# Modulation vectors as dot products on VectorE instead of fp32 matmuls

## The chip, the core and the metric

The kernel runs on one core of a Trainium2 chip. A core has a matrix engine (TensorE, PE in the profile, with PEld for its weight loads), three elementwise engines (VectorE or DVE, ScalarE or ACT, GpSimd or POOL) and a queue engine (SyncE or SP) that issues the DMAs here. PE reads on-chip memory (SBUF) and writes to the accumulation banks (PSUM). The metric is the device time of one execution in microseconds, lower is better.

## What is computed

Two transformer-like blocks, two layers each, over 256 tokens of 1024 features, all in fp32. The change lies in the first block, where each layer begins with six modulation vectors of 1024 per stream, of a stream `x` and a stream `ctx`:

```python
for l in range(DEPTH):                       # DEPTH = 2
    with_ctx = l < DEPTH - 1
    mod_x = (silu(c) @ w_ada[l] + b_ada[l])         # w_ada[l]: [1024, 6144]
    mod_c = (silu(c_ctx) @ w_ada[l] + b_ada[l])
    sh1, sc1, gt1, sh2, sc2, gt2 = split(mod, 6)    # of each stream
    hx = rms_norm(x, g_norm1[l]) * (1 + sc1_x) + sh1_x        # hc alike
    # q, k, v of three mixers = hx @ w_in[l], hc @ w_in[l]; attention over both streams' keys
    x = x + gt1_x * (concat(mixers a, b, c) @ w_out[l])
    hx2 = rms_norm(x, g_norm2[l]) * (1 + sc2_x) + sh2_x
    x = x + gt2_x * conv_ffn(hx2, ...)
    # and ctx likewise, if with_ctx
```

`c` and `c_ctx` are single vectors, so each modulation row is a matrix-vector product with 25 MB of weights per layer.

## The kernel before

A large product is made exact in three passes: `K.weights` (line 153) loads weight tiles of 128 x 1024 (`wraw`, five slots, one 512 KB DMA each on SP's queue, line 144) and `K.split` (255) makes a high part `wh` on ACT (line 259) and a low part `wl` on DVE (line 260); PE then runs high x high, high x low and low x high (lines 178 to 180).

The modulation rows of a layer come from `Block1.ada` (line 305). It is a generator of 24 steps: three banks of 2048 columns (`[sh1|sc1]`, `[gt1|sh2]`, `[sc2|gt2]`), eight 128-row blocks each. A step loads two `wraw` tiles and runs four fp32 matmuls of 32 columns x 512, side by side on the array (line 318; the trace shows each as two records). The stationary operand holds 16 copies of each stream's silu(c). After eight steps DVE adds the bias to the row (323), four transposes turn it into columns (343), DVE copies or scales the columns (353, 355), and gate rows are written to DRAM (326), from where `gate_rows` (360) loads them onto all partitions.

`layer` (line 753) chains the generators of both layers as `self.side`. Eight steps run at the very start, ahead of everything that needs sh1 and sc1; the others run one at a time at each `tick()`: after a 256-column chunk of the input projection (`qb kb vb`, mixer b, `qa0 qa1 kava`, mixer a, `qc kc vc`, mixer c, in the order of `STEPS`), and after each pair of heads in a mixer. All 48 steps of both layers are over before layer 0's FFN.

The program is written in this order, but a scheduler issues it: of the instructions ready on an engine it takes the one written first, by its own estimate of the times, and fixes the order of every engine at compile time. On the chip each engine works strictly in that order. Attention of a head is: scores on PE (533), row maximum on DVE (542), exp on ACT (546), reciprocal and scaling on DVE (594, 553), transposes on PE (558), copy on ACT (560), product with v on PE (574). The second norm (`norm_to`, 219) feeds the FFN through DVE and ACT (265, 268, 269).

Of the kernel before, what the change touches and what calls it, by code (L numbers as in the profile page):

```python
# [50 lines left out]
class Core:  # L51
    def __init__(self, ctx, tc):
# [100 lines left out]
    def weights(self, flat, key, layer, k0, nk, starts, width, piece=1024):  # L153
        """columns (start, k, col) of a weight block as exact (high, low) float32r parts"""
# [27 lines left out]
    def rsqrt(self, parts, n, inv_n):  # L182
        """(sum(parts) * inv_n + EPS) ** -0.5, n columns"""
# [12 lines left out]
        # a cubic step and Newton's, each short of a factor: s goes from -1 to -8/3 to 1024/27, which cancels big ** -0.5  # L196
# [58 lines left out]
    def split(self, src, h, l, gain=None, shift=None):  # L255
        """src (PSUM or SBUF, fp32) * gain + shift -> h + l."""
# [15 lines left out]
    def transpose_split(self, blocks, dsts):  # L272
        """blocks: SBUF [P, P] pieces -> dsts (h, l) [P, P * len(blocks)]"""
# [8 lines left out]
class Block1:  # L282
# [21 lines left out]

    def ada(self, l):
# [3 lines left out]
        m = self.mod[l] = {}  # L309
        gn = self.gn[:, l]  # L310
        for b in range(3):
            bias = K.tile([P, 512], F32, "bada")
            nc.sync.dma_start(bias, self.ap["bada"][l, b])
            ps = K.bank("ada")
            for k in range(KD):
                raw = K.raw(f"w1_{l}", "w_ada", l, k, 1, [b * 2048 + g * 512 for g in range(4)], 512)
                for g in range(4):
                    nc.tensor.matmul(ps[32 * g : 32 * g + 32, :], self.cT[:, k].rearrange("p s r -> p (s r)"), raw[g // 2][0][:, g % 2 * 512 : g % 2 * 512 + 512],  # L318
                                     start=(k == 0), stop=(k == KD - 1), tile_position=(0, 32 * g))
                if k < KD - 1:  # L320
                    yield
            row = K.tile([P, 512], F32, "junk")
            nc.vector.tensor_tensor(row, ps, bias, op=ALU.add)
            if b:
                self.rows[l, b] = K.dram.tile([8, 512], F32, name=f"row_{l}_{b}")
                nc.sync.dma_start(self.rows[l, b], row[0 : P : 16, :])
# [428 lines left out]
    def layer(self, l):  # L755
# [788 lines left out]
```

## Time and profile before

| what | value |
|---|---|
| device time, median of 3 runs | 2211.74 us (2209.02 to 2217.74) |
| span of the profiled execution (first to last instruction) | 2206.8 us |
| what lies around the span: median less span | 4.9 us |
| PE busy | 2121.0 us (96%) |
| DVE busy | 1491.9 us (68%) |
| ACT busy | 1073.9 us (49%) |
| DMA | 331.63 MB, mean 150 GB/s |

Busy time of an engine is the union of its instructions; matmuls are pipelined, so PE at 100% says that something was always in flight. Layer 0 of the first block takes 0 to about 760 us of the span: the first modulation rows to 31, projections and mixers to 354, the output projection to 402, the second norm to 420, the FFN to 760. Everything after that contains no modulation work.

### The profile page before, as it was taken

Reading aid. Unit: us, or ns where it says so; the run is one execution under the profiler, and the core shown is the slowest. Engines: PE = TensorE matmul, PEld = TensorE weight load, DVE = VectorE, ACT = ScalarE, POOL = GpSimd, SP = SyncE. Lnnn points to the kernel's source line nnn. Section 1 sums busy time; section 2 is a strip of 40 time slices with the busy share of each in tenths; the row PEclk is TensorE's granted clock in tenths of the full one; section 3 lists DMA queues with packets and bytes.
Section 4 is the critical chain, followed back from the end, with each engine's and each line's share of the span. In section 5 each row is a group of like instructions: output and inputs, shape, how many; then the busy total and the mean of one; then the engine's idle time right before and its main releaser. Section 6 shows DMA issues by size and latency. Waiting matters only on the chain.

```text
span 2206.8 us, 35818 instructions
## 1 busy us (share of the span) xinstructions
PE 2121.0 (96%) x14204; PEld 1859.2 (84%) x14204; DVE 1491.9 (68%) x3008; ACT 1073.9 (49%) x1841; POOL 0.8 (0%) x7
## 2 busy tenths in 40 slices
PE   6999999899999999998999999998998999998998
PEld 3785667788888898788998899998997999997997
DVE  5663556855556686678777889866555879976454
ACT  4443453532333364566556644455444654454443
POOL 0000000000000000000000000000000000000000
PEclk9998999899999998999999999999999999999999
DMA  9344555322323331034554445554553545554662
GB/s 342 110 163 138 187 189 177 136 76 97 108 77 124 104 99 53 25 123 164 176 200 160 153 163 192 191 182 145 190 184 127 172 153 163 184 190 145 189 183 76
DMA packets 94839, 331.63 MB, mean 150 GB/s; under 512 B 10928, under 2 KB 11312, under 8 KB 94544
## 3 DMA queue, kind: packets, MB, share of 16 engines
q1 hardware_dynamic: 94672, 329.35, 45.5%
q8 instruction: 111, 1.82, 0.3%
q14 instruction: 56, 0.46, 0.1%
HBM read 328.20 MB, written 1.11 MB: 149 GB/s over the span
## 4 chain that ended last, share of the span: by engine, by line
PE 91%; DVE 6%; ACT 2%; DMA 1%; issue 1%; DVEq 0%; ACTq 0%
PE ps L178 17%; PE ps L179 17%; PE ps L180 16%; PE acc L178 6%; PE acc L179 6%; PE acc L180 6%; PE ps L533 4%; PE ada L318 3%; PE o L574 2%; PE ps L558 2%; PE ada L179 1%; PE ada L178 1%; PE ada L180 1%; PE o L179 1%; PE o L178 1%; PE o L180 1%
## 5 line engine op out<-in xcount | busy, mean ns | idle before, releaser
L178 PE MATMUL ps<-T,wh 128*128 128x256 f32 (+1 forms) x2640 | 787.4, 299 | 1.1 <-ACT T L262 1.1
L179 PE MATMUL ps<-T,wh 128*128 128x256 f32 (+1 forms) x2640 | 785.8, 298 | 0.4 <-DVE T L263 0.4
L180 PE MATMUL ps<-T,wl 128*128 128x256 f32 (+1 forms) x2640 | 784.5, 298 | 0.0
L260 DVE TENSOR_TENSOR wl<-wraw,wh 128x1024 fp32r<-128x1024 f32 (+1 forms) x514 | 608.8, 1201 | 157.6 <-ACT wh L259 90.8
L259 ACT CAST wh<-wraw 128x1024 fp32r<-128x1024 f32 (+1 forms) x514 | 515.8, 1031 | 234.6 <-PE ps L179 77.4
L178 PEld LDWEIGHTS ps<-T,wh 128*128 128x128 f32 x2640 | 506.1, 192 | 18.5 <-ACT T L262 2.1
L179 PEld LDWEIGHTS ps<-T,wh 128*128 128x128 f32 x2640 | 506.4, 192 | 17.3 <-DVE T L263 1.3
L180 PEld LDWEIGHTS ps<-T,wl 128*128 128x128 f32 x2640 | 506.2, 192 | 13.8
L178 PE MATMUL acc<-wh,T 128*128 128x256 f32 (+1 forms) x988 | 314.2, 319 | 3.5 <-ACT T L265 3.1
L179 PE MATMUL acc<-wl,T 128*128 128x256 f32 (+1 forms) x988 | 313.1, 318 | 2.3 <-DVE wl L260 2.3
L180 PE MATMUL acc<-wh,T 128*128 128x256 f32 (+1 forms) x988 | 311.5, 316 | 0.3 <-DVE T L269 0.3
L178 PEld LDWEIGHTS acc<-wh,T 128*128 128x128 f32 x988 | 190.3, 193 | 19.4 <-ACT T L265 3.5
L180 PEld LDWEIGHTS acc<-wh,T 128*128 128x128 f32 x988 | 189.9, 192 | 14.7 <-DVE arena L189 1.3
L179 PEld LDWEIGHTS acc<-wl,T 128*128 128x128 f32 x988 | 190.6, 193 | 13.9 <-DVE wl L260 3.0
L542 DVE TENSOR_REDUCE arena<-ps 128x1 f32<-128x512 f32 (+1 forms) x100 | 67.5, 686 | 78.9 <-PE ps L533 78.5
L1141 DVE SCALAR_TENSOR_TENSOR arena<-arena 128x241 f32<-128x241 f32 (+14 forms) x240 | 113.2, 474 | 3.7
L259 ACT CAST T<-arena 128x256 fp32r<-128x256 f32 (+2 forms) x128 | 58.8, 468 | 96.3 <-PE ps L179 26.7
L533 PEld LDWEIGHTS ps<-T,T 128*128 128x128 f32 (+2 forms) x320 | 59.3, 200 | 54.1 <-issue 29.2
L533 PE MATMUL ps<-T,T 128*128 128x256 f32 (+2 forms) x320 | 100.9, 386 | 2.1 <-ACT T L517 2.1
L318 PE MATMUL ada<-wraw,arena 128*32 128x512 f32 x384 | 86.9, 636 | 11.6 <-DVE arena L293 8.3
L546 ACT ACTIVATE arena<-ps,arena 128x512 f32<-128x512 f32 (+1 forms) x120 | 73.6, 620 | 48.1 <-DVE arena L542 37.5
L260 DVE TENSOR_TENSOR T<-arena,T 128x256 fp32r<-128x256 f32 (+2 forms) x128 | 63.2, 501 | 48.8 <-ACT T L259 48.4
(226 smaller groups left out, 2219.1 us busy)
## 6 DMA issues: line engine op xcount, KB each, us to landing
wraw<-w SPq DMA_DIRECT2D x586, 512.0 KB, 4.0
wraw<-w SPq DMA_DIRECT2D x22, 256.0 KB, 2.9
xo<-row SPq DMA_DIRECT2D x12, 256.0 KB, 6.2
v<-xin SPq DMA_DIRECT2D x4, 512.0 KB, 8.5
arena<-rpb SPq DMA_DIRECT2D x8, 256.0 KB, 2.7
v<-post SPq DMA_DIRECT2D x4, 512.0 KB, 4.4
arena<-bada SPq DMA_DIRECT2D x6, 256.0 KB, 5.4
arena<-bc SPq DMA_DIRECT2D x2, 768.0 KB, 4.0
```

Source lines behind the costliest of these rows:

```text
L178: mm(out, ah, bh, start=start, stop=False)
L179: mm(out, ah, bl, start=False, stop=False)
L180: mm(out, al, bh, start=False, stop=stop)
L259: a = nc.scalar.copy(h, src)
L260: b = nc.vector.tensor_tensor(l, src, h.bitcast(F32), op=ALU.subtract)
L318: nc.tensor.matmul(ps[32 * g : 32 * g + 32, :], self.cT[:, k].rearrange("p s r -> p (s r)"), raw[g // 2][0][:, g % 2 * 512 : g % 2 * 512 + ...
L533: self.nc.tensor.matmul(ps[:, col : col + 256], a[:, c], b, start=(n == 0), stop=(n == len(q[s]) - 1))
L542: nc.vector.tensor_reduce(m, ps.rearrange("p (t k) -> p t k", t=nt), axis=AX, op=ALU.max, negate=True)
L546: nc.scalar.activation(p[:, c], ps[:, c], AF.Exp, bias=m[:, i : i + 1], accum_out=tot[:, i : i + 1])
L558: nc.tensor.transpose(ps[:, b * P : b * P + P], p[:, b * P : b * P + P], K.ident)
L574: self.nc.tensor.matmul(out[64 * i : 64 * i + 64, t * P : t * P + P], v[:, k, cols[i] : cols[i] + 64], pts[i][:, b * P : b * P + P], start ...
L1141: yield v.scalar_tensor_tensor(y[:, lo:hi], zs[j][:, lo + t - 15 : hi + t - 15], self.cfw[:, j, t : t + 1], y[:, lo:hi], op0=ALU.mult, op1 ...
```

## The change

The first shift and scale of layer 0 stay fp32 matmuls (`ada_first`, eight steps). All other modulation values are dot products on DVE: the weights are laid out so that 128 outputs lie on the partitions and the 1024 inputs along the row, silu(c) and silu(c_ctx) are broadcast to all partitions once (`crow`), and one `scalar_tensor_tensor` (line 351 of the changed file) multiplies a 128 x 1024 weight tile with a row and writes the 128 sums as a column (`accum_out`). Its product goes to a scratch tile that nobody reads.

```diff
+    def crows(self):
+        self.crow = K.tile([P, 2, D], F32, "crow")
+        nc.sync.dma_start(self.crow, self.ap["crow"].partition_broadcast(P))
+        nc.scalar.activation(self.crow, self.crow, AF.Silu)
...
+    PARTS = dict(sh1=0, sc1=8, gt1=16, sh2=24, sc2=32, gt2=40)
     def ada(self, l):
-        for b in range(3):
-            ps = K.bank("ada")
-            for k in range(KD):
-                raw = K.raw(f"w1_{l}", "w_ada", l, k, 1, [b * 2048 + g * 512 for g in range(4)], 512)
-                for g in range(4):
-                    nc.tensor.matmul(ps[32 * g : 32 * g + 32, :], self.cT[:, k]..., raw[g // 2][0][...], ...)
-                yield
...
+        for name, b0 in self.PARTS.items():
+            if name in m or (name == "sc1" and "a1" in m):
+                continue
+            streams = (0, 1) if l == 0 or name in ("sh1", "sc1") else (0,)
+            for b in range(b0, b0 + 8):
+                ((w, _),) = K.raw(f"w1_{l}", "w_ada_t", l, b, 1, [0], D)
+                for s in streams:
+                    nc.vector.scalar_tensor_tensor(K.tile([P, D], F32, "unread"), w, 1.0, self.crow[:, s],
+                                                   op0=ALU.mult, op1=ALU.mult, accum_out=vals[s][:, b : b + 1])
+                if b == b0 + 7:
+                    for s in streams:
+                        self.part(l, name, s, vals[s][:, b0 : b0 + 8], gn)
+                yield
+    def part(self, l, name, s, v, gn):
+        b0 = self.PARTS[name]
+        nc.vector.tensor_tensor(v, v, self.badac[l][:, b0 : b0 + 8], op=ALU.add)
+        if name[:2] == "gt":
+            row = self.rows[l, int(name[2]), s] = K.dram.tile([1, D], F32, ...)
+            nc.sync.dma_start(row.rearrange("o (b p) -> p (o b)", p=P), v)
+            return
...
@@ layer
-            self.side = chain(*(self.ada(i) for i in range(self.depth)))
-            front = [K.normed(self.x[0]), None]
-            for _ in range(KD):
-                self.tick()
+            front = [K.normed(self.x[0]), None]
+            self.ada_first()
+            self.crows()
+            self.side = chain(*(self.ada(i) for i in range(self.depth)))
@@ layer, FFN of layer 0
                 for j in part:
                     F[j] = self.ffn_up(l, j, XT, n)
+                    self.tick()
+                    self.tick()
```

`part` adds the bias (`badac`, laid as columns); a gate's column goes to DRAM as a row of 1024 (line 366 of the changed file), from where `gate_rows` loads it onto all partitions as before.

A step is now one tile of 128 outputs: 32 steps for layer 0 (two dot products each) and 48 for layer 1 (16 with two, 32 with one), 128 dot products in all. The 38 ticks of the mixers of layer 0 take the first 38 steps, 76 dot products; the ticks in the FFN take the others. Weight bytes are the same as before.

The instructions move as follows. DVE, ahead of the first row maximum of mixer a: `L465`, `L466` and the `L453` to `L462` group are the norm and rope of q and k, `L209` to `L211` the steps of a reciprocal square root. Before, these rows follow each other up to there:

```order
L466 TENSOR_TENSOR xo_1498<-arena,xo_1498 128x8x64
L211 SCALAR_TENSOR_TENSOR arena<-arena 128x8
L465 TENSOR_TENSOR arena<-arena 128x512
L466 TENSOR_TENSOR xo_1517<-arena,xo_1517 128x8x64
L459 TENSOR_TENSOR arena<-arena 128x4x32
L460 TENSOR_TENSOR arena<-arena 128x4x32
L453 TENSOR_REDUCE arena<-arena 128x4
L461 TENSOR_TENSOR arena<-arena 128x256
```

In the changed kernel the last rows ahead of that maximum (`L576`) are (`L351` are dot products, the `L499` and `L500` rows the old `L465` and `L466`):

```order
L1013 TENSOR_SCALAR arena<-arena 128x124
L210 SCALAR_TENSOR_TENSOR arena<-arena 128x4
L351 SCALAR_TENSOR_TENSOR arena<-wraw_2065,arena 128x1024
L211 SCALAR_TENSOR_TENSOR arena<-arena 128x4
L1015 TENSOR_SCALAR arena<-arena 128x32
L351 SCALAR_TENSOR_TENSOR arena<-wraw_2065,arena 128x1024
L499 TENSOR_TENSOR arena<-arena 128x256
L351 SCALAR_TENSOR_TENSOR arena<-wraw_2109,arena 128x1024
L500 TENSOR_TENSOR xo_1657<-arena,xo_1656 128x256
L351 SCALAR_TENSOR_TENSOR arena<-wraw_2109,arena 128x1024
L351 SCALAR_TENSOR_TENSOR arena<-wraw_2149,arena 128x1024
L576 TENSOR_REDUCE arena<-ps_1686 128x1
```

Dot products have come in between. Counted over the whole order, 19 of them stand ahead of the first maximum of mixer b, 24 more ahead of that of mixer a (one of them among mixer b's own rows), 28 more ahead of that of mixer c (7 among mixer a's rows) and 5 more ahead of the first weight split of the output projection. The other DVE rows between these marks are nearly those of before.

DVE in the second norm of layer 0 (`L232` scales x, `L189` to `L202` the reciprocal square root, `L268` and `L269` the modulated splits that the FFN waits for). Before:

```order
L232 TENSOR_SCALAR xo_3904<-arena 128x512
L200 SCALAR_TENSOR_TENSOR arena<-arena 128x1
L201 SCALAR_TENSOR_TENSOR arena<-arena 128x1
L202 SCALAR_TENSOR_TENSOR arena<-arena 128x1
L232 TENSOR_SCALAR xo_3973<-v_307_2887,arena 128x512
L191 SCALAR_TENSOR_TENSOR arena<-arena 128x1
L323 TENSOR_TENSOR arena<-ada_3131,arena 128x512
L268 TENSOR_SCALAR arena<-ps_3905,arena 128x256
```

and after the change:

```order
L197 TENSOR_SCALAR arena<-arena 128x1
L362 TENSOR_TENSOR arena<-arena 128x8
L202 SCALAR_TENSOR_TENSOR arena<-arena 128x1
L198 SCALAR_TENSOR_TENSOR arena<-arena 128x1
L232 TENSOR_SCALAR xo_3791<-v_274_2759,arena 128x512
L199 SCALAR_TENSOR_TENSOR arena<-arena 128x1
L362 TENSOR_TENSOR arena<-arena 128x8
L351 SCALAR_TENSOR_TENSOR arena<-wraw_4017,arena 128x1024
L268 TENSOR_SCALAR arena<-ps_3723,arena 128x256
```

Of the row add of the third bank (`L323`) nothing is left, and six dot products stand between the first reciprocal square root and the last split.

SP's queue between the weight tiles of `vb` and those of `qa0`. Before, `wraw_711` and `wraw_713` are one modulation step, 721 and 723 `vb`, 912 to 961 two modulation steps:

```order
L144 DMA wraw_711<-w_0 128x1024
L144 DMA wraw_713<-w_0 128x1024
L144 DMA wraw_721<-w_0 128x1024
L144 DMA wraw_723<-w_0 128x1024
L144 DMA wraw_912<-w_0 128x1024
L144 DMA wraw_914<-w_0 128x1024
L144 DMA wraw_959<-w_0 128x1024
L144 DMA wraw_961<-w_0 128x1024
L588 DMA arena<-rpb 128x512
```

After the change 715 and 717 are `vb`, 906 to 1140 seven tiles for dot products, 1146 and 1148 `qa0`:

```order
L144 DMA wraw_715<-w_0 128x1024
L144 DMA wraw_717<-w_0 128x1024
L144 DMA wraw_906<-w_0 128x1024
L144 DMA wraw_949<-w_0 128x1024
L144 DMA wraw_993<-w_0 128x1024
L144 DMA wraw_1040<-w_0 128x1024
L144 DMA wraw_1083<-w_0 128x1024
L144 DMA wraw_1127<-w_0 128x1024
L144 DMA wraw_1140<-w_0 128x1024
L144 DMA wraw_1146<-w_0 128x1024
L144 DMA wraw_1148<-w_0 128x1024
```

A tile's slot comes free when DVE has used it, so the loads of `qa0` stand behind the dot products.

## Rows read from the trace of the kernel before

**Rows 1.** The profile page, span, busy times, the chain that ended last

```profile
span 2206.8 us, 35818 instructions
...
PE 2121.0 (96%) x14204; PEld 1859.2 (84%) x14204; DVE 1491.9 (68%) x3008; ACT 1073.9 (49%) x1841; POOL 0.8 (0%) x7
...
PE 91%; DVE 6%; ACT 2%; DMA 1%; issue 1%; DVEq 0%; ACTq 0%
PE ps L178 17%; PE ps L179 17%; PE ps L180 16%; PE acc L178 6%; PE acc L179 6%; PE acc L180 6%; PE ps L533 4%; PE ada L318 3%; PE o L574 2%; PE ps L558 2%; PE ada L179 1%; PE ada L178 1%; PE ada L180 1%; PE o L179 1%; PE o L178 1%; PE o L180 1%
```

**Rows 2.** Windows of all engines, busy us by stretch, clock, DMA

```profile
core 0: us, PE busy (x) PEld busy (x) DVE busy (x) ACT busy (x) POOL busy (x), PEclk, DMA share, GB/s
0.00:31.00 31.00, 17.90 (x91) 5.43 (x92) 9.90 (x74) 9.92 (x19) 0.84 (x7) 1.00 0.94 359
31.00:84.00 53.00, 49.25 (x368) 43.37 (x366) 38.59 (x120) 31.56 (x58) 0.00 (x0) 0.94 0.45 166
84.00:122.00 38.00, 37.73 (x250) 20.94 (x249) 21.60 (x55) 19.92 (x49) 0.00 (x0) 1.00 0.59 204
122.00:168.00 46.00, 43.61 (x354) 40.38 (x351) 31.01 (x104) 19.61 (x37) 0.00 (x0) 1.00 0.40 137
168.00:256.00 88.00, 87.93 (x495) 46.85 (x495) 35.35 (x92) 38.14 (x95) 0.00 (x0) 0.90 0.44 145
256.00:299.00 43.00, 42.65 (x375) 40.53 (x370) 25.82 (x77) 21.54 (x44) 0.00 (x0) 1.00 0.60 205
299.00:354.00 55.00, 52.89 (x300) 27.13 (x298) 34.29 (x115) 30.13 (x85) 0.00 (x0) 1.00 0.66 214
354.00:402.00 48.00, 47.13 (x392) 46.50 (x396) 35.19 (x90) 10.86 (x18) 0.00 (x0) 1.00 0.35 114
402.00:420.00 18.00, 8.61 (x53) 6.26 (x45) 16.12 (x63) 12.96 (x30) 0.00 (x0) 0.66 0.70 235
420.00:760.00 340.00, 340.00 (x1497) 281.15 (x1497) 202.71 (x276) 131.06 (x166) 0.00 (x0) 1.00 0.31 99
```

**Rows 3.** Windows of line 318 alone, the fp32 modulation products

```profile
31.00:84.00 53.00, 4.69 (x16) 0.62 (x16) 0.94 0.45 166
84.00:122.00 38.00, 9.25 (x56) 1.36 (x56) 1.00 0.59 204
122.00:168.00 46.00, 3.46 (x21) 0.45 (x18) 1.00 0.40 137
168.00:256.00 88.00, 24.55 (x102) 3.29 (x102) 0.90 0.44 145
256.00:299.00 43.00, 2.13 (x16) 0.31 (x16) 1.00 0.60 205
299.00:354.00 55.00, 26.28 (x96) 3.58 (x96) 1.00 0.66 214
```

**Rows 4.** Groups by form, count, busy us, mean ns, idle before

```profile
L260 DVE TENSOR_TENSOR wl<-wraw,wh 128x1024 fp32r<-128x1024 f32 x494 | 595.6, 1222 | 154.0 <-ACT wh L259 90.8 <-PE ps L180 27.6 <-issue 12.5
...
L546 ACT ACTIVATION_READ_ACCUMULATOR arena<-ps,arena 128x1 f32 x120 | 24.4, 203 | 0.0
...
L260 DVE TENSOR_TENSOR wl<-wraw,wh 128x512 fp32r<-128x512 f32 x20 | 13.5, 687 | 3.6 <-PE ps L180 2.8 <-PE acc L179 0.7
...
L641 DVE SCALAR_TENSOR_TENSOR arena<-arena 128x512 f32<-128x512 f32 x16 | 11.9, 744 | 0.1
```

**Rows 5.** Timeline of DVE, start us, us, instruction [idle before <-releaser]

```profile
29.96 0.69 DVE L323 TENSOR_TENSOR arena<-ada,arena 128x512 f32<-128x512 f32 x1 [1.62 <-PE ada L318]
...
426.01 3.49 DVE L260 TENSOR_TENSOR wl<-wraw,wh 128x1024 fp32r<-128x1024 f32 x3
```

**Rows 6.** Timeline of PE, first projection and first scores of mixer a

```profile
34.43 0.58 PE L178 MATMUL acc<-wh,T 128*128 128x256 f32 x1 [3.07 <-ACT T L265]
...
167.12 0.89 PE L512 MATMUL ps<-ident_r,xo 128*128 128x128 f32 x6 [1.65 <-ACT xo L486]
```

**Rows 7.** Windows after that 1.65 us gap

```profile
170.00:185.00 15.00, 15.00 (x37) 6.07 (x37) 5.73 (x14) 3.12 (x8) 0.00 (x0) 0.50 0.43 141
```

More of the change, by code (lines that the diff above doesn't have):

```diff
@@ L303, in load_small, with ada_first @@
         self.sm = {k: sm[:, a:b] for k, (a, b) in SM1.items()}
+    def ada_first(self):
+        K, nc = self.K, self.nc
+        gn = self.gn[:, 0]
+        bias = K.tile([P, 512], F32, "bada")
+        nc.sync.dma_start(bias, self.ap["bada"])
+        ps = K.bank("ada")
+        for k in range(KD):
+            raw = K.raw("w1_0", "w_ada", 0, k, 1, [g * 512 for g in range(4)], 512)
+            for g in range(4):
+                nc.tensor.matmul(ps[32 * g : 32 * g + 32, :], self.cT[:, k].rearrange("p s r -> p (s r)"), raw[g // 2][0][:, g % 2 * 512 : g % 2 * 512 + 512],
+                                 start=(k == 0), stop=(k == KD - 1), tile_position=(0, 32 * g))
+        row = K.tile([P, 512], F32, "junk")
+        nc.vector.tensor_tensor(row, ps, bias, op=ALU.add)
+        v = self.ada_cols(row)
+        self.mod[0] = dict(sh1=self.mod_col(v[:, 0:2]), a1=self.mod_col(v[:, 2:4], gn[:, 0:8]))
@@ new lines, in crows @@
+    def crows(self):
+        K, nc = self.K, self.nc
+        self.crow = K.tile([P, 2, D], F32, "crow")
+        nc.sync.dma_start(self.crow, self.ap["crow"].partition_broadcast(P))
+        nc.scalar.activation(self.crow, self.crow, AF.Silu)
+        self.badac = []
+        for l in range(self.depth):
+            self.badac.append(K.tile([P, 48], F32, "badac"))
+            nc.sync.dma_start(self.badac[l], self.ap["badac"][l])
+    PARTS = dict(sh1=0, sc1=8, gt1=16, sh2=24, sc2=32, gt2=40)
@@ L305, in ada @@
     def ada(self, l):
         K, nc = self.K, self.nc
[L309 removed]
+        m = self.mod.setdefault(l, {})
         gn = self.gn[:, l]
[L311 to L334 removed]
@@ new lines, in ada @@
+        vals = [K.tile([P, 48], F32, "adav") for _ in range(2)]
+        for name, b0 in self.PARTS.items():
[5 more added lines that the diff above has]
+                for s in streams:
+                    nc.vector.scalar_tensor_tensor(K.tile([P, D], F32, "unread"), w, 1.0, self.crow[:, s], op0=ALU.mult, op1=ALU.mult,
+                                                   accum_out=vals[s][:, b : b + 1])
+                if b == b0 + 7:
+                    for s in streams:
+                        self.part(l, name, s, vals[s][:, b0 : b0 + 8], gn)
+                yield
@@ new lines, in part @@
+    def part(self, l, name, s, v, gn):
+        K, nc = self.K, self.nc
+        b0 = self.PARTS[name]
+        nc.vector.tensor_tensor(v, v, self.badac[l][:, b0 : b0 + 8], op=ALU.add)
+        if name[:2] == "gt":
+            row = self.rows[l, int(name[2]), s] = K.dram.tile([1, D], F32, name=f"row_{l}_{name}_{s}")
+            with nc.allow_non_contiguous_dma(reason="a column to a row"):
+                nc.sync.dma_start(row.rearrange("o (b p) -> p (o b)", p=P), v)
+            return
+        if name[:2] == "sc":
+            nc.vector.scalar_tensor_tensor(v, v, 1.0, gn[:, 0:8] if name == "sc1" else gn[:, 8:16], op0=ALU.add, op1=ALU.mult)
+        self.mod[l].setdefault("a" + name[2] if name[:2] == "sc" else name, []).append(v)
@@ L362, in gate_rows @@
         out = K.xo()
-        for j in range(2):
-            a = 2 * (2 * (n - 1) + j) + s
-            self.nc.sync.dma_start(out[:, j * 512 : j * 512 + 512], self.rows[l, n][a : a + 1, :].to_broadcast([P, 512]))
+        self.nc.sync.dma_start(out, self.rows[l, n, s].to_broadcast([P, D]))
         return out
@@ L852, in layer @@
             K.norm_to(self.x[s], XT, s * 256, mod["a2"][s], mod["sh2"][s], site=f"n2{l}")
-        for _ in self.side:
-            pass
-        gates = {s: self.gate_rows(l, 2, s) for s in streams}
+        gates = {}
         if full:
@@ L873, in layer @@
                         self.add_gated(self.x[t // 2][t % 2][:, cc * 512 : cc * 512 + 512], ps[t], gates[t // 2][:, cc * 512 : cc * 512 + 512])
+            for _ in self.side:
+                pass
         else:
+            gates = {0: self.gate_rows(l, 2, 0)}
             ps = dict(zip([(t, cc) for t in tts for cc in range(2)], K.acc4()))
@@ L1479, in _pack @@
         if (key, layer) not in done:
-            w = inputs["w_in_2" if key == "w_kr_2" else key][layer]
+            w = inputs[{"w_kr_2": "w_in_2", "w_ada_t": "w_ada"}.get(key, key)][layer]
+            if key == "w_ada_t":
+                w = w.T
             done[key, layer] = w[:, perms[key]] if key in perms else w
@@ L1512 @@
     arrays["gn"] = np.stack([np.concatenate([_cols(i["g_norm1"][l], KD), _cols(i["g_norm2"][l], KD)], axis=1) for l in range(2)], axis=1)
-    arrays["bada"] = np.stack([np.repeat(i["b_ada"][l].reshape(3, 4, 1, 512), 32, axis=2).reshape(3, P, 512) for l in range(2)])
+    arrays["bada"] = np.repeat(i["b_ada"][0, :2048].reshape(4, 1, 512), 32, axis=1).reshape(P, 512)
+    arrays["badac"] = np.stack([_cols(i["b_ada"][l], 48) for l in range(2)])
+    arrays["crow"] = np.concatenate([i["c"][0], i["c_ctx"]])
     arrays["rpb"] = np.stack([_rpb_tiles(i["rpb_b"][l]) for l in range(2)])
```

12 lines of the change are left out of this document (3 added, 9 removed).

## The prediction

> **What bounds the kernel now.** I read the page first. PE is busy for 2121.0 of 2206.8 us, and the chain that ended last is 91% PE, 6% DVE [rows 1]; the reader is to see that `ada L318`, the work removed, is 3% of that chain, some 66 us. Next the windows by stage, since 96% is an average: from 31 us to the output projection at 354 PE is busy for 313.2 of 323 us (49.25 + 37.73 + 43.61 + 87.93 + 42.65 + 52.89), DVE for 186.7 (38.59 + 21.60 + 31.01 + 35.35 + 25.82 + 34.29), and in the FFN PE is busy for all of 340.00 us and DVE for 202.71 [rows 2]. Line 318 by itself has 70.4 us there, 4.69 + 9.25 + 3.46 + 24.55 + 2.13 + 26.28 [rows 3]. Last the forms and timelines, for prices. The profiled execution lasted 2206.8 us between first and last instruction; the measured median is 4.9 us more, and I add these 4.9 to a span. The PE order behind layer 0's FFN is the same in both kernels, so all that changes lies before 760 us.
>
> **What goes.** PE loses 70.4 us between 31 and 354 us, which leaves 313.2 − 70.4 = 242.8, and about 2 us more in the output projection and the second norm, where PE waits for DVE and ACT anyway (8.61 busy of 18.00 us [rows 2]).
>
> **The price of a dot product.** The trace shows no DVE instruction that accumulates. The nearest row is a product of two fp32 tiles by the same instruction at half the length, 744 ns for 128x512; a DVE pass of the other kind costs 687 at 512 columns and 1222 at 1024, so 512 columns more are 535, and 744 + 535 = 1279 ns [rows 4]. Packed densely, three such passes take 3.49 us, 1.163 each [rows 5] instead of 1.222, so 1279 − 59 = 1220 is the lower end. If the sum is written by a second instruction, the nearest row is the readout of ACT's accumulator, 203 ns [rows 4]: 1279 + 203 = 1482 is the upper end. I take 1.35 us, in the middle, since rows on DVE and on ACT are about equally far from it.
>
> One rule speaks against this price. The Trainium skill, "Vector Engine (DVE) Microarchitecture Reference", section "Points that are easy to get wrong", says that this instruction with two SBUF sources that aren't bf16 runs at half throughput, as no read port is left for the accumulator. The row of 744 ns has two fp32 SBUF sources and is 57 ns over the 687 of a plain pass, so no halving shows where nothing is accumulated; with accumulation no run here shows it. It is a rival below.
>
> **What it adds, stage by stage.** 76 dot products fall in 31 to 354 us: 76 × 1.35 = 102.6 on DVE, 289 with the 186.7, against 243 of PE. By sums alone DVE would still fit into 323 us. But DVE works in order, and the dot products stand ahead of the row maxima that PE's scores, exp and transposes hang on. So the bound moves to DVE in the stretches ahead of a mixer, and to PE inside one. The stages (ends of before: 31, 84, 122, 168, 256, 299, 354):
>
> - Front. `crow` (128 × 2048 × 4 bytes, 1 MB) and another 0.5 MB tile now go to the queue ahead of the last projection tile, and the layer's small table of 0.35 MB (688 columns) goes behind it: 1.05 + 0.52 − 0.35 = 1.22 MB at the 359 GB/s that the front shows [rows 2] is 3.4 us. PE's first projection product, at 34.43 [rows 6], comes some 3 us later; I start DVE at 34.
> - To the first maximum of mixer b (19 dot products): DVE 38.6 + 19 × 1.35 = 64.3, and 3 us of waits for PE and ACT, to 101 (84 before).
> - Mixer b: PE 37.7 − 9.25 = 28.5. Before mixer a the granted clock stands at 0.50, the lower of its levels (1.2 GHz), for 15 us [rows 7] after a stretch of thin PE work that ends with a wait of only 1.65 us [rows 6]. Longer waits ahead of mixers b and a make such a fall likely in each; I add 7 us, half of that stretch being lost. Against it DVE runs free while PE works off mixer b and does some 8 us of the next stage's rows. 27.5, to 128.5.
> - To the maximum of mixer a (1 + 23 dot products): DVE 31.0 + 23 × 1.35 = 62.1, to 190.5 (168 before).
> - Mixer a: PE 87.93 − 24.55 = 63.4, 8 of DVE's run-ahead off as above, 55.4, to 246. The 7 dot products in its rows are covered, DVE being busy for 35.35 of 88.
> - To the maximum of mixer c (21): DVE 25.8 + 28.4 = 54.2, to 300 (299 before).
> - Mixer c and projection chunk tail: DVE 34.3 + 5 × 1.35 = 41, with 3 us of waits, 44; PE has 52.9 − 26.3 = 26.6 and is covered. To 344 (354 before): 10 us won.
> - Output projection: 3 dot products beside 47 us of PE, covered. DVE has 35.19 there [rows 2]; with 4 more it still fits.
> - Second norm: six dot products in the chain, 6 × 1.35 = 8.1, less the row add of 0.69 [rows 5] and 1.9 of idle that they fill: 5.5 lost. This one stands in the open, PE having nothing else.
> - FFN: 43 × 1.35 = 58 on DVE, 261 of 340 us, where PE is busy for all 340 [rows 2]. Splits of weights come a little late at times; 2 us, from 0 to 8 (8 is six dot products met by PE without cover).
>
> Sum: −10 + 5.5 + 2 = −2.5 against 2206.8, a span of 2204.3, and with 4.9 about 2209 us. Beside these, ACT's pass over `crow` lies in the front, where ACT has 9.92 of 31 us [rows 2], and the bias adds take 8 columns where the old row add had 512 (0.69 us [rows 5]): I take 0 for both, and at most that 0.69 for each of the four adds ahead of the maxima if they find no gap. The gate's row, written from a column in 1024 pieces of 4 bytes, is no row of this trace. Its readers come after mixer c, a stage of 55 us [rows 2] that hides it; I take 0, and 7 if the weights queued behind it on SP are held up.
>
> The sum says: PE gives up 72 us, DVE's queue takes 70 of them back. What is least sure is the overlap, so both sides stay open.
>
> **The rivals.**
> 1. Faster. The dot product costs the lower end, 1.22, and fills the gaps between the short norm and rope instructions, where DVE is idle for 136 us (323 − 186.7). Then the three stretches ahead of the maxima shrink by 63 × 0.13 = 8 us, the two clock losses or waits (7 and 3) vanish, and the second norm loses 4.5 instead of 5.5; with another 7 us of run-ahead, 2209 − 8 − 10 − 1 − 7 = 2183. For it: that idle time is 42% of the mixers. Against it: idle time between dependent short instructions is only filled by what stands there in the order.
> 2. PE stays the bound everywhere, all of the 70.4 are won and the second norm costs nothing: 2140. Against it: DVE's own sum ahead of each maximum is longer than PE's.
> 3. Slower, by one mechanism: DVE as an in-order queue, with no run-ahead during mixers b and a, since the next chunk's tiles wait for `wraw` slots that dot products hold on SP. The two overlaps of 8 us are lost: 2209 + 16 = 2225, past the half per cent by themselves. With 1.48 a dot product ahead of the maxima (63 × 0.13 = 8) and 8 instead of 2 us in the FFN it is 2239, and with the 1.3 of the second norm about 2240. It decides if the first maximum of mixer a comes later than 195 us. For it: before, a split of `qa0` never stood behind a dot product. Against it: five slots, and loads at 45% of the DMA [rows 2].
> 4. A dot product runs at half speed, its accumulation taking turns with its reads: of the 1279 ns, 2 × 535 grow with the columns, and twice that gives 1279 + 1070 = 2349 ns. 73 of the dot products stand where DVE sets the end (63 + 5 + 5 and over), 73 × 1.0 = 73 more: about 2282. For it: no row accumulates on DVE, so none excludes it. Against it: 744 beside 687 [rows 4], two such sources at nearly the speed of a plain pass. (This is what the rule cited from the Trainium skill, "Vector Engine (DVE) Microarchitecture Reference", section "Points that are easy to get wrong", would do here.)
>
> **How the numbers follow.** A measurement of this kernel tells about 0.5%, 11 us, from no change. The forecast has 0.38 (own range 2190 to 2225), rival 1 0.27, rival 2 0.06, rival 3 0.23, rival 4 0.06. The range leaves out rivals 2 and 4 and the outer edges of 1 and 3: 2168 to 2250. Faster than 2201: rivals 1 and 2 and a little of the forecast's lower side, 0.36. Slower than 2223: rivals 3 and 4 with a bit of the forecast, 0.30. Between: 0.34.
>
> **What the profile after would show.** Right: a mean of line 351 between 1.22 and 1.48 us; PE waits that end with DVE ahead of the first maxima, these at about 101 and 190 us, the output projection from about 344; a granted clock under 1 in mixers b and a; a longer PE gap at the second norm; PE still full in the FFN. Wrong: a mean under 1.2 or over 1.5; the first maximum of mixer b before 90 us (rival 1 or 2); PE waits that end with DMA, which the working above has only at the front; or an FFN longer than 348 us, where the dot products there would not be covered.

## The result

The changed kernel takes 2227.5 us (median, 2222.07 to 2230.27); the kernel before took 2210.47 beside it (2208.9 to 2217.74). The ratio is 1.0067, 95% interval 1.0046 to 1.0088: slower, by 17 us. The forecast was 2209. What has to be found is where the 72 us of PE work went that the change takes away.

The page of the changed kernel answers to [rows 1]:

```profile
span 2220.3 us, 35410 instructions
...
PE 2087.5 (94%) x13864; PEld 1879.1 (85%) x13864; DVE 1615.8 (73%) x3268; ACT 1071.0 (48%) x1842; POOL 0.8 (0%) x7
...
PE 83%; DVE 11%; ACT 2%; DMA 2%; issue 2%; SPq 0%; DVEq 0%; ACTq 0%
```

PE has lost 33.5 us of busy time (2121.0 − 2087.5), not 72, and DVE has 11% of the chain instead of 6%. The same stretches as in [rows 2], now of the changed kernel (columns as there):

```profile
31.00:84.00 53.00, 41.53 (x289) 37.08 (x286) 47.38 (x153) 27.01 (x50) 0.00 (x0) 0.81 0.60 211
84.00:122.00 38.00, 34.22 (x213) 28.80 (x211) 29.25 (x67) 20.20 (x42) 0.00 (x0) 0.87 0.47 125
168.00:256.00 88.00, 74.92 (x446) 53.60 (x445) 62.43 (x166) 44.45 (x110) 0.00 (x0) 0.83 0.25 74
299.00:354.00 55.00, 39.25 (x162) 33.92 (x162) 34.49 (x106) 26.15 (x73) 0.00 (x0) 0.50 0.24 60
402.00:420.00 18.00, 12.21 (x94) 12.01 (x94) 17.86 (x68) 7.12 (x18) 0.00 (x0) 0.85 0.20 55
420.00:760.00 340.00, 331.87 (x1454) 273.80 (x1453) 251.74 (x371) 129.75 (x169) 0.00 (x0) 0.98 0.52 161
```

The reader is to look at the third column from the end, the granted clock of TensorE (1.00 is 2.4 GHz, 0.50 is 1.2 GHz). In 299 to 354 us, where it was 1.00 before, it is 0.50, and PE is busy for 39.25 us with 162 instructions, where it did 300 in 52.89. Over the whole program the mean clock fell. Of the changed kernel:

```profile
core 0: 2220.3 us, clock 0.950
```

and of the kernel before:

```profile
core 0: 2206.8 us, clock 0.976
```

(1 − 0.976) × 2206.8 = 53 us of full-speed time were withheld before, (1 − 0.950) × 2220.3 = 111 us now, 58 us more. The loss lies ahead of 760 us, where the mean fell from 0.98 to 0.90; behind that it is 0.98 in both. Of the 72 us that PE gave up, the clock took back up to 58: an upper bound, since a part of the withheld time falls into PE's waits.

The stages are read from the first row maximum of each mixer (DVE) and from PE: the first product of the projections, the first high x low product behind mixer c's last product with v (column "out. proj."; single products of the output projection can stand earlier, between the heads of mixer c), and the first product of the FFN. One profile each, in us:

| kernel | first product | max b | max a | max c | out. proj. | FFN | span |
|---|---|---|---|---|---|---|---|
| before | 34.4 | 85.9 | 169.7 | 300.0 | 354.8 | 419.9 | 2206.8 |
| forecast | 37.9 | 101 | 190.5 | 300 | 344 | 414.5 | 2204.3 |
| after | 42.5 | 102.8 | 188.7 | 302.2 | 364.7 | 432.6 | 2220.3 |
| e1_row | 43.5 | 102.6 | 189.4 | 303.4 | 359.8 | 427.8 | 2215.4 |
| e2_warm | 45.5 | 106.2 | 190.3 | 303.5 | 367.6 | 436.7 | 2225.9 |
| e3_both | 45.5 | 104.4 | 188.4 | 301.9 | 358.3 | 427.4 | 2216.7 |
| e4_short | 42.2 | 104.6 | 196.6 | 303.7 | 349.6 | 393.6 | 2185.8 |
| e5_short_row | 41.7 | 95.7 | 179.7 | 287.7 | 333.6 | 381.6 | 2172.3 |
| e6_late | 42.7 | 93.7 | 188.3 | 330.4 | 401.2 | 465.4 | 2258.7 |
| e7_late_crow | 34.3 | 85.1 | 175.5 | 315.2 | 386.0 | 450.2 | 2243.4 |
| e8_warm_pt | 43.9 | 102.7 | 189.5 | 309.5 | 363.5 | 424.9 | 2212.0 |
| e9_split | 35.8 | 86.7 | 170.9 | 282.2 | 328.8 | 395.3 | 2184.0 |
| e10_early | 36.0 | 87.4 | 171.2 | 296.9 | 340.0 | 393.2 | 2181.0 |
| e11_row_crow | 35.8 | 95.1 | 181.5 | 297.6 | 355.2 | 420.3 | 2208.2 |
| e12_row_crow_warm | 34.1 | 92.3 | 184.3 | 300.4 | 359.3 | 416.8 | 2204.4 |
| e13_cap26 | 34.1 | 93.0 | 180.1 | 290.8 | 332.3 | 387.1 | 2180.2 |

(The forecast's FFN is 344 plus the 65.0 us from output projection to FFN of before plus 5.5.) Up to mixer c the forecast holds within 2.2 us at each maximum. From there to the output projection it had 44 us, and 62.5 passed. What PE waits for (timeline of the changed kernel's PE, [rows 6] before):

```profile
42.46 0.58 PE L178 MATMUL acc<-wh,T 128*128 128x256 f32 x1 [5.06 <-ACT wh L259]
...
314.05 0.80 PE L178 MATMUL acc<-wh,T 128*128 128x256 f32 x2 [8.18 <-ACT wh L259]
...
316.39 1.97 PE L686 MATMUL o<-v,arena 128*128 128x64 f32 x8 [0.69 <-ACT arena L594]
```

Two waits stand out: 5.06 us ahead of the first projection, and 8.18 us in mixer c, both for ACT. The product that waits in mixer c is one of the output projection; it stands between the heads in PE's fixed order, so the heads behind it wait too. But ACT in the second had itself been idle:

```profile
312.95 1.04 ACT L259 CAST wh<-wraw 128x1024 fp32r<-128x1024 f32 x1 [7.93 <-DMA wraw<-w]
```

for the DMA of a weight tile. A gate's row went through the queue ahead of it:

```profile
292.35 0.38 SPq L366 DMA_DIRECT2D row_gt<-arena  x1
...
298.49 7.04 SPq L144 DMA_DIRECT2D wraw<-w  x3
```

All six writes of such rows:

```profile
L366 SPq DMA_DIRECT2D row_gt<-arena x6: 378/422/567, 93.9 to 713.8; - x6
...
DMA to landing us min/median/max: 10.0/12.4/13.4
```

4 KB that take 12.4 us to land in the median (a weight tile of 512 KB lands in 3.8). The DMA columns at the end of these windows show what it does to others:

```profile
297.00:305.00 8.00, 5.67 (x30) 4.70 (x30) 7.90 (x16) 5.33 (x13) 0.00 (x0) 0.61 0.47 36
305.00:313.00 8.00, 0.80 (x2) 0.50 (x2) 1.83 (x5) 0.07 (x2) 0.00 (x0) 0.50 0.98 314
```

In the first 8 us the DMA engines are busy for 47% and move 36 GB/s, in the next, with what was queued behind the row, they move 314. The line `316.39 1.97` above is the other half: the eight products with v take 1.97 us at a clock of 0.50. In the kernel before, at 1.00:

```profile
319.18 1.11 PE L652 MATMUL o<-v,arena 128*128 128x64 f32 x8
```

### The profile page after: what moved, and what is told of

Its sections match the earlier page's. It is cut to its first block, busy times and chain, and to the rows that moved or that the text cites. A ratio compares the mean times of both kernels' runs of the same rounds, so it can differ in the third digit from the quotient of the medians.

```text
span 2220.3 us, 35410 instructions
## 1 busy us (share of the span) xinstructions
PE 2087.5 (94%) x13864; PEld 1879.1 (85%) x13864; DVE 1615.8 (73%) x3268; ACT 1071.0 (48%) x1842; POOL 0.8 (0%) x7
## 4 chain that ended last, share of the span: by engine, by line
PE 83%; DVE 11%; ACT 2%; DMA 2%; issue 2%; SPq 0%; DVEq 0%; ACTq 0%
PE ps L178 16%; PE ps L179 16%; PE ps L180 16%; PE acc L178 5%; PE acc L179 5%; PE acc L180 5%; PE ps L567 4%; DVE arena L351 2%; PE o L608 2%; PE ps L592 2%; DMA wraw<-w 2%; PE o L686 1%; DVE wl L260 1%; PE ada L179 1%; PE ada L180 1%
## 5 line engine op out<-in xcount | busy, mean ns | idle before, releaser
L178 PE MATMUL acc<-wh,T 128*128 128x256 f32 (+1 forms) x988 | 318.8, 324 | 14.0 <-ACT wh L259 13.2
L180 PE MATMUL acc<-wh,T 128*128 128x256 f32 (+1 forms) x988 | 314.8, 320 | 0.0
L178 PEld LDWEIGHTS acc<-wh,T 128*128 128x128 f32 x988 | 193.9, 197 | 28.1 <-ACT wh L259 13.9
L180 PEld LDWEIGHTS acc<-wh,T 128*128 128x128 f32 x988 | 192.9, 195 | 12.8 <-issue 0.6
L351 DVE SCALAR_TENSOR_TENSOR arena<-wraw,arena 128x1024 f32<-128x1024 f32 x128 | 155.7, 1217 | 10.7 <-DMA wraw<-w 10.3
L567 PE MATMUL ps<-T,T 128*128 128x256 f32 (+1 forms) x320 | 107.1, 415 | 4.5 <-ACT T L551 2.5
L1388 DVE TENSOR_TENSOR arena<-arena,ps 128x256 f32<-128x256 f32 x44 | 18.5, 421 | 113.7 <-ACT arena L1387 113.7
L576 DVE TENSOR_REDUCE arena<-ps 128x1 f32<-128x512 f32 (+1 forms) x100 | 67.4, 684 | 44.1 <-PE ps L567 43.5
L567 PEld LDWEIGHTS ps<-T,T 128*128 128x128 f32 (+1 forms) x320 | 65.1, 225 | 38.4 <-issue 13.8
L1387 ACT ACTIVATE arena<-ps 128x256 f32<-128x256 f32 x44 | 16.9, 384 | 156.3 <-PE ps L180 156.3
```

The costliest lines, as they stand in the source:

```text
L178: mm(out, ah, bh, start=start, stop=False)
L180: mm(out, al, bh, start=False, stop=stop)
L351: nc.vector.scalar_tensor_tensor(K.tile([P, D], F32, "unread"), w, 1.0, self.crow[:, s], op0=ALU.mult, op1=ALU.mult, accum_out=vals[s][:, ...
L567: self.nc.tensor.matmul(ps[:, col : col + 256], a[:, c], b, start=(n == 0), stop=(n == len(q[s]) - 1))
L576: nc.vector.tensor_reduce(m, ps.rearrange("p (t k) -> p t k", t=nt), axis=AX, op=ALU.max, negate=True)
```

## The experiments

Ratios are against the kernel before, on the same chip, with 95% intervals. All began from the changed kernel, except e9 and e10, which began from the one before.

**The write and the clock.** e1 writes the gate's row in pieces of 512 bytes:

```diff
-            with nc.allow_non_contiguous_dma(reason="a column to a row"):
-                nc.sync.dma_start(row.rearrange("o (b p) -> p (o b)", p=P), v)
+            ps = K.bank()
+            nc.tensor.transpose(ps[:8, :P], v, K.ident)
+            t = K.tmp()[:8, :P]
+            nc.scalar.copy(t, ps[:8, :P])
+            nc.sync.dma_start(row.rearrange("o (b p) -> (o b) p", p=P), t)
```

> The changed kernel, but a gate's column is turned into 8 rows of 128 by one PE transpose and an ACT copy, and written to DRAM in 8 pieces of 512 bytes instead of 1024 pieces of 4 bytes. Theory (the write clogs the DMA engines): its landing falls from 12.4 us to under 4, the PE wait of 8.18 us at 306 us is gone, and the time falls by 8 to 12 us, to 2215 to 2219. Rival (the clock alone): mixer c stays at a granted clock of 0.50, the wait goes but what is behind it is late anyway; 0 to 4 us, 2223 to 2228. Rival (DVE's load alone): no change, 2227.

2216.89 us, ratio 1.0025 (1.0014 to 1.0036), 10.6 us under the changed kernel: the theory's range (how fast the new row lands, this trace does not show). The wait of 8.18 us became 0.79:

```profile
307.91 0.79 PE L178 MATMUL acc<-wh,T 128*128 128x256 f32 x2 [0.79 <-ACT wh L259]
...
310.25 1.97 PE L689 MATMUL o<-v,arena 128*128 128x64 f32 x8 [0.69 <-ACT arena L597]
```

but the same products still take 1.97 us, and the rest of mixer c stays at half clock:

```profile
303.00:360.00 57.00, 46.74 (x193) 39.91 (x193) 39.89 (x123) 29.29 (x84) 0.00 (x0) 0.50 0.16 52
```

56.4 us of mixer c remain, which the rival of the clock had said. e2 and e3 were to lift that clock with unread matmuls at the ticks of mixer c, without and with e1's edit:

> The changed kernel, with two fp32 matmuls of 32 x 512 that nobody reads added at each of the 12 ticks of mixer c, about 1 us of PE each tick at full clock. Theory (the clock: without the modulation products PE is too idle in mixer c and stays at 0.50): granted clock in mixer c rises from 0.50 to over 0.8, first maximum of c to output projection falls from 62.5 us to 45 to 52, time 2212 to 2219 in spite of 12 us more PE work. Rival (the row write or DVE sets mixer c): clock or not, 62 us or more, 2227 to 2240.

> Both edits: the row by a transpose, and the unread matmuls in mixer c. If the two causes are separate and add, 2204 to 2211, with mixer c 38 to 45 us. If the wait for DMA is what drops the clock (one cause), the same time as the row edit alone or up to 6 us slower, since PE does 12 us more. If DVE's load sets all, 2227.

2226.88 us, 1.0078 (1.0065 to 1.0090), and 2216.25 us, 1.0026 (1.0015 to 1.0036): as without them. They tested nothing, since these matmuls wait for nothing that mixer c makes. In e3 (durations, then first and last start):

```profile
L378 PE MATMUL ada<-arena x48: 589/592/1060, 38.1 to 54.2; 128*32 128x512 f32 x48
```

they all ran before 55 us. e8 makes them wait for each head's probabilities:

```diff
+                nc.tensor.matmul(self.spare[0:32, :], self.cT[:, 0], pt, start=True, stop=True, ...)
             self.tick()
```

> The row in pieces of 512 bytes, and one unread fp32 matmul of 32 x 512 on each head's transposed probabilities in mixer c (the unread matmuls tried before had no such input and ran at 42 to 60 us instead, so they tested nothing). Clock theory: granted clock in mixer c over 0.8, first maximum to output projection 56.4 us falls to 44 to 50, time 2205 to 2211. Rival (PE's clock does not set mixer c, or one more matmul doesn't raise it): 0.50 and 56 to 70 us, 2217 to 2230.

2214.81 us, 1.0009 (0.9995 to 1.0022). The clock comes back (L694 is the unread matmul; with the third line begin the products of the output projection that e1 does not have there):

```profile
318.24 1.92 PE L694 MATMUL ada<-arena 128*32 128x512 f32 x2
322.89 1.04 PE L694 MATMUL ada<-arena 128*32 128x512 f32 x2
343.70 0.39 PE L179 MATMUL acc<-wl,T 128*128 128x256 f32 x1
```

The windows of mixer c:

```profile
309.00:325.00 16.00, 11.49 (x42) 6.96 (x42) 12.60 (x32) 8.12 (x20) 0.00 (x0) 0.68 0.33 114
325.00:363.00 38.00, 35.55 (x216) 24.61 (x215) 31.62 (x98) 22.31 (x65) 0.00 (x0) 1.00 0.22 63
```

It is 1.00 from 325 us on, where e1 had 0.50 to the end, and that some 18 us ahead of these products. That PE with too little to do is what holds the clock down in mixer c is thereby shown; that it pays is not, as the interval overlaps e1's. Mixer c took 54.0 us, not 44 to 50: the unread work, 13.4 us of PE there, takes most of what the clock gives.

**DVE's time.** e4 leaves the dot products at 32 of 1024 columns, e5 the same with e1's edit:

```diff
-  scalar_tensor_tensor(K.tile([P, D], F32, "unread"), w, 1.0, self.crow[:, s], ...)
+  scalar_tensor_tensor(K.tile([P, D], F32, "unread")[:, :32], w[:, :32], 1.0, self.crow[:, s, :32], ...)
```

> The changed kernel with each dot product over 32 of its 1024 inputs, so the modulation values are left incomplete; loads, waits and the row writes stay, and DVE gets some 1.1 us less for each of 128. Theory (DVE in order ahead of the first maxima): the first maxima of mixers b, a and c come 15 to 25, 35 to 45 and 50 to 70 us earlier; the time falls by 50 to 75 us less what the lower clock takes, 2150 to 2185. Rival (DMA or clock set these stretches): under 20 us, 2207 or more.

2187.81 us, 0.9899 (0.9885 to 0.9912), and the maxima did not come earlier; what was won lies behind them, 16.6 us in mixer c and 23.9 from there to the FFN (rows e4_short and after of the table). The theory looked refuted ahead of the maxima, but DVE was waiting:

```profile
91.08 0.19 DVE L351 SCALAR_TENSOR_TENSOR arena<-wraw,arena 128x32 f32<-128x32 f32 x1 [6.58 <-DMA wraw<-w]
```

With shorter instructions the scheduler placed the row write and more tiles ahead of mixer b, so that the write's queue replaced DVE's time there.

> Dot products over 32 of the 1024 inputs (modulation values incomplete), and the gate's row written in pieces of 512 bytes. With short dot products alone the first maxima did not come earlier (104.6, 196.6, 303.7 us), and DVE waited there for weight tiles behind the row write. Theory (DVE's time, hidden there by the write): now the first maxima of b, a, c come before 92, 165 and 270 us and the time is 2145 to 2175. Rival (the loads of the weight tiles themselves, or the order, set them): still over 100, 185 and 295, and 2178 to 2190.

2174.9 us, 0.9851 (0.9833 to 0.9870). Against e1 42.0 us less, for about 132 us of DVE time taken away (128 × 1.03, a dot product of 32 columns taking 0.18 to 0.19 us instead of 1.22). The maxima came 6.9, 9.7 and 15.7 us earlier than in e1, less than the theory had; the clock in 85 to 105 us was 0.72. By the table another 10.5 us were won in mixer c and 20.0 from the output projection to the FFN. The scheduler has set a new order as well: of line 178's products in the output projection (about 128) some 30 lie in mixer c here, 3 in e1. So DVE's time, together with the order that it leads to, is shown as a cost of some 42 us; what either is worth by itself isn't.

**Where they stand.** e6 makes dot products only at the heads, and pins each on DVE behind its head's row maximum (with e1's edit; 60 in the mixers):

```diff
+                    K.queue(ins, self.top)        # self.top: the row maximum of the head
...
+            self.left = 30                        # steps in the mixers
...
-            if name != "qb":
-                self.tick()
```

> Row in pieces of 512 bytes, and the dot products made only at the ticks of heads, each queued on DVE behind the row maximum of its head, so that none stands ahead of the first maximum of mixer b, 2 between mixers b and a and 2 between a and c; 60 in the mixers, 68 in the FFN instead of 76 and 52. Theory (DVE's in-order queue ahead of the maxima is the cost): first maxima at 86 to 92, 150 to 160, 240 to 260 us, time 2165 to 2190. Rival (the dot products cost the same wherever they stand, now inside the mixers): maxima earlier, but output projection within 8 us of the 359.8 us with the row edit alone, 2208 to 2222. Rival (the FFN can't cover 68): FFN over 348 us.

2256.91 us, 1.0205 (1.0191 to 1.0220): worse than any theory said. The first maximum of mixer b comes 8.9 us earlier than in e1, and mixer a is lost. Mixer a of e6, and then of the changed kernel:

```profile
188.00:281.00 93.00, 86.68 (x340) 56.71 (x340) 53.25 (x124) 33.49 (x84) 0.00 (x0) 0.56 0.20 58
```

```profile
189.00:252.00 63.00, 63.00 (x376) 43.82 (x375) 39.34 (x97) 35.14 (x88) 0.00 (x0) 0.89 0.16 49
```

340 instructions in 86.68 us of PE at a clock of 0.56, against 376 in 63.00 at 0.89. A dot product pinned inside a head lengthens that head's chain: PE is idle for 6.3 of the 93 us, in eight waits at the products with v above all, where the changed kernel has no wait in mixer a. The clock goes down on top, and with it PE's busy time grows by 23.7 us.

> As the one before, and the 1 MB load of the broadcast silu rows moved on SP's queue behind the first projection weights and the second stream's tokens. If that load is what delays the front (first projection product at 43 us instead of 34), it comes at 35 to 39 and the time is 4 to 8 us lower than without the move. If something else delays it, within 2 us.

2240.91 us, 1.0135 (1.0121 to 1.0149), 16.0 us better, where 4 to 8 were expected: more than the 8.4 us by which the first product came earlier, and the rest is not explained. e11 does the same without e6's pinning:

```diff
-        nc.sync.dma_start(self.crow, self.ap["crow"].partition_broadcast(P))
+        K.queue(nc.sync.dma_start(self.crow, ...), K.last)   # behind the first projection's weights
...
+            if full and name == "kb":
+                self.crows()
```

> The changed kernel with the row in pieces of 512 bytes and the broadcast silu rows loaded behind the first projection weights. First projection product at 35 us instead of 43; if the front's delay passes through to the end, 2216.9 falls to 2203 to 2209; if DVE's queue ahead of mixer b eats it, 2213 to 2217.

2207.86 us, 0.9981 (0.9971 to 0.9990), 9.0 us under e1 and within the expected range: without the slow write and the early load of `crow` the changed kernel is level with the one before. PE's first projection product is back near the 34.43 of [rows 6]:

```profile
35.80 0.58 PE L178 MATMUL acc<-wh,T 128*128 128x256 f32 x1 [3.07 <-ACT T L265]
```

> The one before with the unread matmul on each head's probabilities in mixer c. If the clock there is worth what the last such run showed (a median 2.1 us under the row edit, with the clock back at 1.00 from 325 us on), 1 to 6 us under the kernel without it; if not, the same or slower.

2203.82 us, 0.9967 (0.9953 to 0.9981): 4.0 us less, intervals overlapping, not clear.

**Without them in the mixers.** e9 and e10 keep layer 0's modulation on PE and make layer 1's 64 dot products inside layer 0's FFN:

```diff
-            self.side = chain(*(self.ada(i) for i in range(self.depth)))
+            self.side = self.ada(0)
...
+            self.side = self.dots(1)           # at the FFN; two or three steps after each ffn_up
```

> The kernel before, with layer 0's modulation as fp32 matmuls on PE, as it was, and layer 1's as 64 dot products on DVE, all inside layer 0's FFN. Layer 0's 16 steps lie at the 6 ticks of mixer b, ahead of qc and kc, and at 9 heads of mixer c, none in mixer a or the other chunks. Theory (a dot product costs only where PE waits for DVE, and fp32 matmuls keep the clock up where PE would be idle): mixers a and the chunks lose some 30 us of PE work (24.6 + 4.7 + 3.5), clock in mixers b and c at 0.95 or more, FFN under 346 us; 2180 to 2195. Rival (the 64 dot products hold up the FFN): FFN over 355 us, 2200 or more. Rival (the clock falls in mixer a without them): mixer a stays at 75 us or more, 2200 or more.

> As the one before, but layer 0's 16 steps lie at the chunks, mixer b and the first heads of mixer a, so mixer c has no fp32 products and DVE no dot products either. Clock theory: mixer c has 26 us of PE work in 55, its clock falls to 0.50 and it takes 50 us or more from its first maximum to the output projection, as long as with the products (54.8), so this kernel is 5 to 15 us slower than the one before. Rival (mixer c was lengthened by DVE's dot products and DMA only): clock 0.9 or more, mixer c 35 to 42 us, and 2165 to 2185.

e9: 2186.61 us, 0.9884 (0.9867 to 0.9901), in the expected range, with a clock of 1.00 in mixer c but 0.85 in mixer b (87 to 122 us). e10: 2184.04 us, 0.9874 (0.9858 to 0.9889), in the rival's range. In e10 mixer c has no fp32 products and took 43.1 us:

```profile
297.00:340.00 43.00, 41.45 (x327) 39.42 (x326) 36.46 (x120) 29.75 (x84) 0.00 (x0) 0.96 0.10 32
```

So the clock theory in its simple form (no fp32 products, hence 0.50) fell. Beside e1, e10 has no dot products in the mixers at all, and fp32 products up to mixer a. e13 stays with the changed kernel (with e11's edits) and moves 24 dot products to the FFN, some 20 of which stood between mixer a's last maximum and mixer c's first:

```diff
     def tick(self):
-        next(self.side, None)
+        self.left -= 1
+        if self.left >= 0:
+            next(self.side, None)
...
+            self.left = 26                     # steps in the mixers
```

> The changed kernel with the row in pieces of 512 bytes and the silu rows loaded late, and only the first 26 of 38 ticks of the mixers used (52 dot products instead of 76, the other 24 go to the FFN, which has 76): in DVE's order only 2 dot products stand between mixer a's last row maximum and mixer c's first, instead of 22. Theory (dot products ahead of the maxima starve PE, and the starved PE enters mixer c at the lower clock, 0.50, and stays there): first maximum of c at 265 to 280 us instead of 297.6, clock in mixer c 0.95 or more, mixer c 42 to 47 us instead of 57.6, time 2165 to 2185. Rival (the clock falls in mixer c whatever stands ahead of it, for want of fp32 products): first maximum as early, but 0.50 and 55 us or more, 2185 to 2200. Rival (the FFN can't cover 76 dot products): from its first product 8 us or more longer.

2183.41 us, 0.9875 (0.9858 to 0.9891): 24.5 us under e11. Mixer c of e11, with 22 dot products between mixer a's last maximum and its own first, and of e13, with 2:

```profile
298.00:355.00 57.00, 48.98 (x203) 42.65 (x203) 39.47 (x121) 30.14 (x85) 0.00 (x0) 0.50 0.16 53
```

```profile
291.00:332.00 41.00, 38.68 (x312) 36.11 (x310) 35.54 (x120) 30.11 (x85) 0.00 (x0) 1.00 0.10 32
```

57.6 us at 0.50 against 41.5 us at 1.00. PE has 312 instructions in it instead of 203. The added ones are products of the output projection, which the scheduler has drawn forward between the heads; in e11 nearly all of them stand behind mixer c. Line 178 alone (a third of these products), in mixer c and from there to the FFN, of e11:

```profile
297.60:355.20 57.60, 3.24 (x8) 2.35 (x8) 0.50 0.17 55
355.20:420.30 65.10, 34.17 (x121) 23.02 (x120) 0.89 0.33 110
```

and of e13:

```profile
290.80:332.30 41.50, 12.08 (x41) 7.81 (x41) 1.00 0.10 32
332.30:387.10 54.80, 24.24 (x86) 16.41 (x86) 0.86 0.37 120
```

The maximum itself came 6.8 us earlier, not the 17 to 32 expected. Behind it, 16.1 us are won in mixer c and 10.3 from there to the FFN; from the FFN on, with its 76 dot products, 5.2 are lost. e9, e10 and e13 beat both kernels by over 1%.

Is it the entry at the lower clock that holds it at 0.50 through mixer c, or the thin work between the heads? e10 enters at 0.50 too, and leaves it within 8 us:

```profile
297.00:300.00 3.00, 3.00 (x16) 3.00 (x15) 3.00 (x7) 3.00 (x9) 0.00 (x0) 0.50 0.10 36
300.00:305.00 5.00, 5.00 (x43) 4.95 (x42) 3.71 (x11) 2.36 (x6) 0.00 (x0) 0.98 0.01 3
```

In e10 products of the output projection lie between the heads, in e8 unread matmuls; both come back to 1.00. The changed kernel, e1 and e11 enter at 0.50 with next to nothing added, and stay. So the entry alone does not hold the clock down.

## Why the prediction was wrong

The range held the time, but the kernel was forecast 2.5 us faster and is 17 slower. Two terms of the sum failed outright, mixer c and the gate's row, and the front was set too small. By its steps:

- **Price of a dot product**, 1.35 us taken, 1.22 to 1.48 as bounds. The rows of the changed kernel:

```profile
L351 DVE SCALAR_TENSOR_TENSOR arena<-wraw,arena 128x1024 f32<-128x1024 f32 x128 | 155.7, 1217 | 10.7 <-DMA wraw<-w 10.3
...
L351 DVE DVE_READ_ACCUMULATOR arena<-wraw,arena 128x1 f32 x128 | 10.3, 80 | 0.0
```

1217 + 80 = 1297 ns, inside. The sum is written by an instruction of its own, as the upper end supposed, but it costs 80 ns and not 203. Rival 4 is out: 1217 ns beside the 1222 of a plain pass of that length [rows 4]. The rule on halved throughput (the Trainium skill, "Vector Engine (DVE) Microarchitecture Reference", section "Points that are easy to get wrong") is not what this trace shows, with two fp32 SBUF sources and an accumulated sum.
- **Front**: 3.4 us taken, 8.0 measured. The mechanism (the 1 MB of `crow` in the queue) was right, as e11 shows, and it is worth 9.0 us of the time. The size was off: the row add on DVE alone comes 5.6 us later than its 29.96 of [rows 5], and the first projection product, which now waits for a weight cast on ACT (5.06 us, above), loses another 2.4.

```profile
35.54 0.69 DVE L319 TENSOR_TENSOR arena<-ada,arena 128x512 f32<-128x512 f32 x1 [21.52 <-PE ada L316]
```

- **Ahead of mixers b, a and c**: 101, 190.5 and 300, measured 102.8, 188.7 and 302.2. Right in part by luck: e11, without the late front and the slow write, has 95.1, 181.5 and 297.6, so the stretches were set too long, and the two delays filled that up.
- **Mixer c**: 44 us, "PE has 26.6 and is covered". This step failed: 62.5. It reckoned PE's 26.6 us at full clock and DVE's 41 as the bound. At 0.50 the same PE work is 53 us (26.6 / 0.5), and with the waits between the heads mixer c takes 56.4 in e1 and 57.6 in e11, where the slow write is gone; by the profiles 6.1 of the 18.5 us too many are the write's, 12.4 stay. Where the clock was back at 0.96 to 1.00 with products of the output projection between the heads, mixer c took 41.5 (e13) and 43.1 us (e10), about what the step had. I had put the loss of the clock into mixer b (7 us) and not into c, where the profile before showed 1.00 with 26.3 us of fp32 products between the heads.
- **The gate's row**: 0 taken, "a stage of 55 us that hides it", 7 if it holds up the queue. It holds up the queue: 10.6 us (e1). That its readers come late hides only its own data; the weights issued behind it waited. The prediction's own sign of being wrong, a PE wait that goes back to a DMA behind the front, is this one (the 8.18 us above). The Trainium skill, "DMA: Bandwidth & Descriptors", section "Rules for kernel authors", warns against a plain DMA over a rearranged access pattern in place of a transpose; the 12.4 us for 4 KB point the same way, its factor was not measured here.
- **Second norm**: 5.5 us; output projection to FFN took 68.0 us instead of 65.0, so 3.0. **FFN**: 2 us; from its first product to the end 0.7 us more than before (432.65 and 419.86 us to 2220.3 and 2206.8). There the dot products are covered, which is why the FFN is the place for them; even the 76 of e13 cost 5.2 us against e11.
- **From span to median**: 4.9 us added; here the median lies 7.2 above the profiled span, 2.3 of the miss. One run's time lies only 1.8 us above its own span (2222.07 and 2220.3 us); the rest is that the profiled run was the fastest of its five, so the 4.9 are not a fixed cost around the span.
- **PE's sum**: the six windows add up to 314.1 us, not 313.2; no term of the sum hangs on it.

In sum the span missed by 16.0: mixer c 18.5, up to it 2.2, second norm and FFN −3.8 (3.0 and 0.7 instead of 5.5 and 2); the −0.9 that remain are that the forecast set 344 against 354, where the first product of before stood at 354.8. In the medians the miss is about what the slow write and the late front cost, 10.6 and 9.0 us: e11, without either, runs in 2207.86 us, 1 us beside the forecast. That it lands there is luck, since its mixer c takes 57.6 us and not 44; earlier maxima (2.4 us at mixer c) and 5.4 us less from the output projection to the FFN make up for most of that. Rival 3 had the right sign and not the mechanism: the first maximum of mixer a came at 188.7, before the 195 at which it would have decided.

Left open: why the scheduler draws products of the output projection between the heads in e4, e5, e10 and e13 and leaves them behind mixer c in the changed kernel, e1 and e11. No run moves these products with the dot products left in place, so how the 24.5 us of e13 divide between the two is not shown.

## What to carry to other kernels

Work taken from the busy engine can be what filled its waits: before moving it, ask stage by stage what PE will do between the links of the chain, and price the remaining work at the lower clock too. Put the moved work where the receiving engine has slack and the giving one is dense (here the FFN before the change: PE busy for 340 of 340 us, DVE for 203), not ahead of the first link of a chain. A small strided write is not small for what is queued behind it.

## What was not expected of the hardware

- Reading out DVE's accumulator takes 80 ns, and a dot product over 1024 columns of two fp32 tiles 1217 ns, as long as a plain pass.
- The granted clock stayed at 0.50 (1.2 GHz) for 51 us with PE busy for 43.95 of them (314 to 365 us of the changed kernel), in short products with waits of up to 0.7 us between them.
- 1024 pieces of 4 bytes took 10.0 to 13.4 us to land, and the DMA engines moved 36 GB/s in 8 us (297 to 305) behind one of them.
